# A two-layer attention and feed-forward trunk on one core: for two of four query blocks the product of probabilities and v goes into the block's own score bank

## The chip, the core and the metric

The program runs on one core of one Trainium2 chip, in a single launch. The metric is the time of one execution on the device in microseconds (us). Before the change it is 1463.2 us, the median of three runs (1463.0 to 1464.0). The engines are called as in the profile: PE is TensorE with its weight loads PEld, DVE is VectorE, ACT is ScalarE, POOL is GpSimd, SP is SyncE, which only issues DMAs here.

## What is computed

Two layers over 512 positions and 1024 features, all in float32. The core of one layer:

```python
u = (rmsnorm(x, norm1_w) * (1 + sc1) + sh1) @ w_in     # one combined projection
y_pool, y_conv = pool_mixer(u_pool), b_conv * causal_short_conv(c_conv * u_conv)
o = moba_attention(q, k, v)              # 8 heads of 64, blocks of 256 keys
merged = gates0 * (y_pool @ p_pool) + gates1 * (y_conv @ p_conv) + gates2 * (y_attn @ p_attn)
x = x + g1 * (merged @ w_out)
h2 = rmsnorm(x, norm2_w) * (1 + sc2) + sh2
x = x + g2 * ((silu(h2 @ w_gate) * (h2 @ w_up)) @ w_down)
```

For the change only the attention matters. For each head and each block of 128 queries, the scores of the queries against all earlier keys go through a softmax, the probabilities are transposed, and their product with v is the head's output:

```python
p = softmax(concat([s_sel, s_own]))      # a past block of keys counts where its gate is valid
out = p_sel @ v_sel + p_own @ v_own
```

## The kernel before

Features lie on the 128 partitions, positions along the free axis. A float32 product is made of three matmuls in a faster format (`mm3`): each operand is split into a high and a low part, and high·high, high·low and low·high are added up in the same accumulator. Weights arrive by DMA in a tile `raw` of 8 blocks of 128 x 128, ACT rounds them to `whi` (line 327), DVE makes the rest `wlo` (line 330).

The accumulators (PSUM) are eight banks of 512 float32 per partition, in two pools. `ps_mm()` hands out four single banks, shared by everything that is called `mm` in the profile: the projections, gates and branch products, the transposes and, so far, each product of probabilities and v. `ps_pair()` hands out two tiles of two banks each, called `pair`; in the attention these hold scores, one bank for each of the two heads of a head pair.

The attention is cut into units. A head pair (4 in a layer) and a block of 128 queries (`i` = 0 to 3) make one unit, `unit(hp, i, ...)`, a generator in three stages:

- scores: PE adds a mask and three products of 64 rows for each head into `s = ps_pair()`; DVE takes maxima from `s` (lines 598 to 614), ACT makes the exponentials from it (line 601 for `i` below 2, lines 616 and 618 from 2 on), DVE divides by the sum (line 623);
- transposes: PE transposes the probabilities into one `mm` bank for `i` below 2, into two from `i` = 2 on; ACT copies them rounded (line 634), DVE subtracts for the rest (line 635);
- the product with v (the PV product here): 2(i + 1) matmuls of 128 x 256 into one bank `po`; ACT copies part of it (line 648), DVE adds the other parts (lines 649 and 651), ACT and DVE split the sum for the next product (lines 652 and 653).

The stages are woven into other work. Each time some 2048 columns of `mm3` have been issued, `tick()` lets the generators that are due take a step; the rest of the PE stream is the gate products of the merge (`gate()`, read by ACT at line 912) and the branch products (read by DVE at line 917, `gated`). So between the stages of a unit PE works through gates. `attention` also starts each head pair with eight transposes of q and k (`to_features`, read by ACT at line 517 and DVE at line 518).

PE's instructions keep the order in which they are written; weight splits on DVE are pinned to that order too. For the rest, a scheduler with its own idea of durations fixes, when the program is built, the order of instructions on ACT and DVE and which free bank a new tile gets: a tile takes a bank of its pool that was given up early, and its first matmul waits on PE for the last reader of the tile that was there. Each engine works strictly in its order, so an instruction that waits holds everything behind it.

Of the kernel before, what the change touches and what calls it, by code (L numbers as in the profile page):

```python
# [79 lines left out]
def hybrid_trunk(ctx, tc, xT, ws, ada, cols, pool_w, qk_w, crow, pos, con, out):  # L80
# [12 lines left out]
    def nm(s):  # L93
        uid[0] += 1
        return f"{s}{uid[0]}"
# [4 lines left out]
    def tmp():  # L100
        return work.tile([P, S], F32, tag="tmp", name=nm("tmp"), bufs=5)

    def ps_mm():
        return psum.tile([P, S], F32, tag="mm", name=nm("mm"), bufs=4)

    def ps_pair():
        return psum.tile([P, 2, S], F32, tag="pair", name=nm("pair"), bufs=2)

    def w4(shape, dt=F32):
        return work.tile(shape, dt, tag="w4", name=nm("w4"), bufs=6)  # L110

    def sm(shape, dt=F32, tag="sm", bufs=8):
        return small.tile(shape, dt, tag=tag, name=nm(tag), bufs=bufs)
# [36 lines left out]
    def matmul(*a, **k):  # L150
        tc.keep_in_program_order(T.matmul(*a, **k))  # L151
# [4 lines left out]
    def transpose(*a):  # L156
        tc.keep_in_program_order(T.transpose(*a))  # L157
# [422 lines left out]
    def unit(hp, i, q, k, v, y, nrq, prq):  # L580

        w = P * (i + 1)
        wm = max(w, BLOCK)
        s = ps_pair()

        for a in range(2):
            matmul(s[:, a, i * P:w], ident16, mask, start=True, stop=True)
        for z, (qa, ka) in enumerate(((0, 0), (0, 1), (1, 0))):
            for a in range(2):
                r = slice(a * HD, (a + 1) * HD)  # L590
                matmul(s[:, a, :wm], q[qa][r, i * P:(i + 1) * P], k[ka][r, :wm],
                       start=False, stop=(z == 2), skip_group_check=True)
        cell = lambda: sm([P, 2], tag="asm", bufs=16)
        nsc, sc = nrq[:, i, 2 * hp:2 * hp + 2], prq[:, i, 2 * hp:2 * hp + 2]
        m, nb, den = cell(), cell(), cell()
        pr = [tmp() for _ in range(2)]
        if w <= BLOCK:
            V.tensor_reduce(m, s[:, :, :w], axis=AX.X, op=ALU.max)
            V.tensor_mul(nb, m, nsc)
            for a in range(2):  # L600
                A.activation(pr[a][:, :w], s[:, a, :w], AF.Exp, bias=nb[:, a:a + 1],
                             scale=sc[:, a:a + 1], accum_out=den[:, a:a + 1])
        else:

            gs, pen, mp, nbp, d2 = cell(), cell(), cell(), cell(), cell()
            V.tensor_reduce(gs, s[:, :, :BLOCK], axis=AX.X, op=ALU.add)
            V.tensor_mul(gs, gs, sc)
            V.tensor_scalar(pen, gs, NEG * BLOCK * SCALE, NEG, op0=ALU.is_lt, op1=ALU.mult)
            V.tensor_reduce(mp, s[:, :, :BLOCK], axis=AX.X, op=ALU.max)
            V.tensor_add(mp, mp, pen)  # L610
            V.tensor_reduce(m, s[:, :, BLOCK:w], axis=AX.X, op=ALU.max)
            V.tensor_max(m, m, mp)
            V.tensor_mul(nb, m, nsc)
            V.tensor_add(nbp, nb, pen)
            for a in range(2):
                A.activation(pr[a][:, :BLOCK], s[:, a, :BLOCK], AF.Exp, bias=nbp[:, a:a + 1],  # L616
                             scale=sc[:, a:a + 1], accum_out=den[:, a:a + 1])
                A.activation(pr[a][:, BLOCK:w], s[:, a, BLOCK:w], AF.Exp, bias=nb[:, a:a + 1],  # L618
                             scale=sc[:, a:a + 1], accum_out=d2[:, a:a + 1])
            V.tensor_add(den, den, d2)  # L620
        V.reciprocal(den, den)
        for a in range(2):
            V.tensor_scalar(pr[a][:, :w], pr[a][:, :w], den[:, a:a + 1], None, op0=ALU.mult)
        yield WAIT[i]

        pt = [None] * 2
        for aa in ([0, 1],) if i < 2 else ([0], [1]):
            n = len(aa)
            tp = ps_mm().rearrange("p (j a q) -> p j a q", a=n, q=P)[:, :i + 1]
            for a in aa:  # L630
                for j in range(i + 1):
                    transpose(tp[:, j, a - aa[0], :], pr[a][:, j * P:(j + 1) * P], ident)
            both = w4([P, i + 1, n, 2, P], F32R)
            A.activation(both[:, :, :, 0], tp, AF.Copy)
            V.tensor_sub(both[:, :, :, 1], tp, f32(both)[:, :, :, 0])  # L635
            for a in aa:
                pt[a] = both[:, :, a - aa[0]]
        yield 2

        po = ps_mm().rearrange("p (a h q) -> p a h q", a=2, h=2)  # L640
        for a in range(2):
            for j in range(i + 1):
                matmul(po[:, a].rearrange("p h q -> p (h q)"), v[hp // 2][j][:, hp % 2 * 2 + a].rearrange("p h d -> p (h d)"),
                       pt[a][:, j].rearrange("p h q -> p (h q)"), start=(j == 0), stop=(j == i))
        c = slice(i * P, (i + 1) * P)
        t = tmp()
        part, total = t[:HD, :2 * P].rearrange("p (a q) -> p a q", a=2), t[:, 2 * P:3 * P]
        A.activation(part, po[HD:, :, 0], AF.Copy)
        V.tensor_add(part, part, po[:HD, :, 1])
        for a in range(2):  # L650
            V.tensor_add(total[a * HD:(a + 1) * HD], part[:, a], po[:HD, a, 0])
        A.activation(y[0][:, c], total, AF.Copy)
        V.tensor_sub(y[1][:, c], total, f32(y[0])[:, c])
# [6 lines left out]
    def attention(l, qk, v, nrq, prq, y_attn):  # L660

        for hp in range(PAIRS):
            q = to_features(l, qk, 0, hp)
            yield 1
            k = to_features(l, qk, 1, hp)
            y = bigt(), bigt()
            y_attn.append(y)
            yield 2
            for i in range(TT):
                start(unit(hp, i, q, k, v, y, nrq, prq))  # L670
                if i < TT - 1:
                    yield GAP[i]
            yield 1
# [45 lines left out]
    for l in range(L):  # L719
# [7 lines left out]
        for n, (k, lo, hi) in enumerate([(k, 0, S) for k in range(KT)] if l == 0 else HALVES + REST):  # L727
# [18 lines left out]
            h = norm.k(k)  # L746
# [515 lines left out]
```

## Time and profile before

| | |
|---|---|
| median of 3 runs | 1463.2 us (1463.0 to 1464.0) |
| the profiled execution, its own time | 1463.28 us |
| span of its profile, first to last instruction | 1461.5 us |
| matmuls and weight loads on PE | 8443 each |
| attention of layer 0, of layer 1 (about) | 135 to 308 us, 853 to 1030 us |
| POOL busy | 105.8 us |

The span is 1.8 us shorter than the time of the same execution. In a timeline the columns are start (us from the start of the span), duration, engine, line, operation, what is written and read, shapes, and how many instructions in a row are merged; a bracket at the end is idle time of the engine before it and what ended that. Because all matmuls come from one helper, line 151 stands for every product and the tile names tell them apart: `mm<-w,big` is a PV product, `mm<-ident,w` the transposes of q and k, `mm<-ident,tmp` those of the probabilities, `mm<-big,whi` and `mm<-big,wlo` the gates and branch products, `pair<-mask,ident` and `pair<-big,big` the scores. A matmul's recorded duration is longer than the distance to the next one, since they are pipelined; what a place costs is read from starts.

### The profile page before, as it was taken

How to read it: one execution, taken by the hardware profiler on the slowest of the kernel's cores; microseconds unless marked ns; L12 is line 12 of the kernel's file. 1: busy time of each engine (PE TensorE's matmuls, PEld its weight loads, DVE VectorE, ACT ScalarE, POOL GpSimd, SP SyncE). 2: the span in 40 equal slices, each digit the busy share in tenths (PEclk: the TensorE clock that was granted, in tenths of full speed). 3: DMA queues.
4: the chain of work that ended last, by engine and by line, in shares of the span. 5: the costliest groups of instructions: out<-in, count | busy, mean ns of one | idle time of the engine just before them, and what ended most of it. 6: DMA issues, size and time to landing. Idle time of an engine off the chain costs nothing.

```text
span 1461.5 us, 21960 instructions
## 1 busy us (share of the span) xinstructions
PE 1452.0 (99%) x8443; PEld 1268.2 (87%) x8443; DVE 1053.0 (72%) x1855; ACT 665.8 (46%) x1138; POOL 105.8 (7%) x157
## 2 busy tenths in 40 slices
PE   9999999999999999999999999999999999999998
PEld 7888888788989998989988888778889889989997
DVE  7988888748686867677797867766487757657663
ACT  4634555443454452535444355555335525434450
POOL 0000000001100221210000000000020102111200
PEclk9999999999999999999999999999999999999999
DMA  9645334345436766756545421222462436636522
GB/s 347 225 139 174 124 106 142 133 159 151 109 115 205 200 174 203 187 149 201 189 150 177 159 75 71 73 73 102 154 194 78 142 118 167 175 113 185 138 84 84
DMA packets 84409, 217.19 MB, mean 149 GB/s; under 512 B 10832, under 2 KB 23760, under 8 KB 84304
## 3 DMA queue, kind: packets, MB, share of 16 engines
q1 hardware_dynamic: 67456, 177.37, 35.6%
q0 software_dynamic: 16128, 37.76, 11.8%
q8 instruction: 66, 1.08, 0.3%
q10 hardware_dynamic: 720, 0.66, 0.1%
q14 instruction: 39, 0.32, 0.1%
HBM read 213.65 MB, written 2.10 MB: 148 GB/s over the span
## 4 chain that ended last, share of the span: by engine, by line
PE 95%; DVE 3%; ACT 1%; DMA 1%; issue 0%; SPq 0%
PE mm L151 81%; PE pair L151 12%; PE mm L157 2%; DVE wlo L330 1%; ACT whi L327 0%; DMA w<-in_ada 0%; DMA x<-in_xT 0%; DVE w L376 0%; ACT tmp L616 0%; ACT tmp L618 0%; DVE tmp L485 0%; DVE big L504 0%; DVE big L518 0%; DVE big L488 0%; DVE w L635 0%
## 5 line engine op out<-in xcount | busy, mean ns | idle before, releaser
L151 PE MATMUL mm<-big,whi 128*128 128x512 f32 (+1 forms) x4362 | 1081.2, 339 | 1.6 <-DVE big L488 0.9
L151 PEld LDWEIGHTS mm<-big,whi 128*128 128x128 f32 x4362 | 745.7, 190 | 86.9 <-DVE big L488 1.7
L151 PE MATMUL mm<-big,wlo 128*128 128x512 f32 (+1 forms) x2181 | 736.1, 337 | 0.0
L151 PEld LDWEIGHTS mm<-big,wlo 128*128 128x128 f32 x2181 | 413.9, 190 | 44.4
L327 ACT ACTIVATE whi<-raw 128x1024 fp32r<-128x1024 f32 (+2 forms) x240 | 248.8, 1039 | 283.6 <-PE mm L151 207.5
L330 DVE TENSOR_TENSOR wlo<-raw,whi 128x1024 fp32r<-128x1024 f32 (+2 forms) x240 | 283.6, 1192 | 54.5 <-ACT whi L327 54.2
L327 ACT ACTIVATE whi<-w 128x1024 fp32r<-128x1024 f32 x72 | 76.2, 1059 | 145.4 <-PE mm L151 102.0
L957 DVE SCALAR_TENSOR_TENSOR x<-mm,mod,x 128x512 f32<-128x512 f32 (+1 forms) x90 | 61.7, 688 | 83.2 <-PE mm L151 83.1
L256 POOL DMA_DIRECT2D w<-in_ws x72 | 46.9, 661 | 972.8 <-DVE w L376 391.7
L330 DVE TENSOR_TENSOR wlo<-w,whi 128x1024 fp32r<-128x1024 f32 x72 | 86.8, 1221 | 30.4 <-ACT whi L327 29.7
L376 DVE SCALAR_TENSOR_TENSOR w<-w,csil 128x1024 f32<-128x1024 f32 x80 | 95.9, 1219 | 15.7 <-DMA w<-in_ada 15.5
L151 PE MATMUL pair<-whi,big 128*128 128x512 f32 x224 | 76.8, 390 | 0.0
L258 POOL DMA_DIRECT2D w<-in_ws x72 | 65.0, 930 | 145.1 <-DMA w<-in_ws 131.1
L151 PE MATMUL pair<-big,whi 128*128 128x256 f32 (+1 forms) x376 | 74.0, 294 | 0.0
L151 PEld LDWEIGHTS pair<-big,whi 128*128 128x128 f32 x376 | 60.4, 191 | 2.2
L151 PE MATMUL mm<-whi,big 128*128 128x512 f32 x160 | 57.2, 394 | 1.5 <-ACT big L501 1.2
L151 PE MATMUL pair<-big,wlo 128*128 128x256 f32 (+1 forms) x188 | 55.3, 294 | 0.0
L917 DVE SCALAR_TENSOR_TENSOR big<-big,mm 128x512 f32<-128x512 f32 x48 | 32.6, 684 | 26.4 <-PE mm L151 26.1
L151 PEld LDWEIGHTS pair<-whi,big 128*128 128x128 f32 x224 | 42.1, 188 | 8.7
L515 DVE TENSOR_TENSOR big<-tmp,big 128x512 fp32r<-128x512 f32 x48 | 33.0, 691 | 22.4 <-ACT big L514 21.6
L514 ACT ACTIVATE big<-tmp 128x512 fp32r<-128x512 f32 x48 | 29.7, 623 | 36.1 <-DVE tmp L1096 13.2
L151 PE MATMUL pair<-wlo,big 128*128 128x512 f32 x112 | 43.7, 390 | 0.0
(187 smaller groups left out, 1243.1 us busy)
## 6 DMA issues: line engine op xcount, KB each, us to landing
raw<-in_ws SPq DMA_DIRECT2D x146, 512.0 KB, 3.4
w<-in_ada SPq DMA_DIRECT2D x80, 512.0 KB, 5.1
w<-in_ws POOLq DMA_DIRECT2D x144, 256.0 KB, 4.6
raw<-in_ws SPq DMA_DIRECT2D x64, 256.0 KB, 3.5
raw<-in_ws SPq DMA_DIRECT2D x24, 384.0 KB, 3.5
raw<-in_ada SPq DMA_DIRECT2D x16, 512.0 KB, 3.2
raw<-in_ws SPq DMA_DIRECT2D x16, 448.0 KB, 5.6
raw<-in_ws SPq DMA_DIRECT2D x36, 128.0 KB, 3.0
```

Source lines behind the costliest of these rows:

```text
L151: tc.keep_in_program_order(T.matmul(*a, **k))
L157: tc.keep_in_program_order(T.transpose(*a))
L256: nc.gpsimd.dma_start(dst, self.source(0, 1))
L258: nc.gpsimd.dma_start(dst, self.source(*other), accum_op=ALU.add)
L327: A.activation(hi[:, :n], raw[:, :n], AF.Copy)
L330: ins = V.tensor_sub(lo[:, :n], raw[:, :n], f32(hi)[:, :n])
L376: return V.scalar_tensor_tensor(aw, aw, 1.0, csil, op0=ALU.mult, op1=ALU.mult, accum_out=mod[l][:, part, j:j + 1])
L514: A.activation(hi, src, AF.Copy)
L515: last_split[0] = V.tensor_sub(lo, src, f32(hi))
L917: V.scalar_tensor_tensor(sg, sg, 1.0, branch, op0=ALU.add, op1=ALU.mult)
L957: V.scalar_tensor_tensor(x[k][:, lo:hi], src, mod[l][:, part, k:k + 1], x[k][:, lo:hi], op0=ALU.mult, op1=ALU.add)
```

## The change

For the units with `i` = 2 and `i` = 3 the PV product goes into the first bank of the unit's own score tile `s`. For `i` = 0 and 1 it stays in an `mm` bank. What is computed is the same.

```diff
@@ -637,7 +637,8 @@
                 pt[a] = both[:, :, a - aa[0]]
         yield 2
 
-        po = ps_mm().rearrange("p (a h q) -> p a h q", a=2, h=2)
+
+        po = (s[:, 0] if i >= 2 else ps_mm()).rearrange("p (a h q) -> p a h q", a=2, h=2)
         for a in range(2):
             for j in range(i + 1):
                 matmul(po[:, a].rearrange("p h q -> p (h q)"), v[hp // 2][j][:, hp % 2 * 2 + a].rearrange("p h d -> p (h d)"),
```

The rest of the unit, which reads `po`, is unchanged: the copy, the three additions and the split. There are two such units in each head pair, so 16 in the program: 16 tiles fewer are asked of the `mm` pool. In the program as built, PE, POOL and SP issue the same instructions in the same order; on ACT three copies at line 652 stand one place later, on DVE a few instructions change their turn at two places (lines 635, 651 and 653 in layer 0, lines 917 and 932 in layer 1).

One consequence lies in the score pool. Before, the score tiles alternate between the two buffers. After, the buffers of units 2 and 3 stay taken longer; of the next head pair, units 0 and 1 both get the buffer of unit 2, one after the other, and its unit 2 gets that of unit 3.

## The prediction

> **What bounds the kernel now.** The page is read first: the busy shares, the granted clock, the chain that ended last.
>
> ```profile
> span 1461.5 us, 21960 instructions
> PE 1452.0 (99%) x8443; PEld 1268.2 (87%) x8443; DVE 1053.0 (72%) x1855; ACT 665.8 (46%) x1138; POOL 105.8 (7%) x157
> PEclk9999999999999999999999999999999999999999
> ...
> PE 95%; DVE 3%; ACT 1%; DMA 1%; issue 0%; SPq 0%
> ```
>
> PE is the bound, at full clock, and 95% of the chain is its own work. The change takes no matmul away, so it can only give or take waits of PE. The view of waits, kept to PE, lists what ended them; the rows that belong to accumulator banks in the attention are these:
>
> ```profile
> PE mm L151 <- ACT big L912: 1.0, 2, 0.5
> PE mm L151 <- DVE w L635: 0.3, 1, 0.3
> PE mm L151 <- DVE big L917: 0.2, 1, 0.2
> ```
>
> Four waits, 1.5 us in all. That is a lower bound, since a matmul's recorded duration runs into the gap after it. So I read starts in the timeline of PE. Each head pair after the first puts the PV product of unit 2 right behind four transposes (`mm<-ident,w`), and six sites have the same sequence. Four lines for an undisturbed one, then the three that are not:
>
> ```profile
> 168.74 0.60 PE L157 MATMUL mm<-ident,w 128*128 128x128 f32 x4
> 169.09 0.96 PE L151 MATMUL mm<-w,big 128*128 128x256 f32 x6
> 169.88 0.63 PE L151 MATMUL mm<-big,whi 128*128 128x512 f32 x2
> ...
> 253.26 0.60 PE L157 MATMUL mm<-ident,w 128*128 128x128 f32 x4
> 254.05 0.98 PE L151 MATMUL mm<-w,big 128*128 128x256 f32 x6 [0.19 <-DVE big L917]
> 254.86 0.40 PE L151 MATMUL mm<-big,whi 128*128 128x512 f32 x1
> ...
> 929.15 0.60 PE L157 MATMUL mm<-ident,w 128*128 128x128 f32 x4
> 930.29 0.98 PE L151 MATMUL mm<-w,big 128*128 128x256 f32 x6 [0.54 <-ACT big L912]
> 931.11 0.63 PE L151 MATMUL mm<-big,whi 128*128 128x512 f32 x2
> ...
> 972.79 0.60 PE L157 MATMUL mm<-ident,w 128*128 128x128 f32 x4
> 973.87 0.95 PE L151 MATMUL mm<-w,big 128*128 128x256 f32 x6 [0.48 <-ACT big L912]
> 974.66 0.40 PE L151 MATMUL mm<-big,whi 128*128 128x512 f32 x1
> ```
>
> From the first transpose to the first gate matmul the undisturbed site takes 169.88 − 168.74 = 1.14 us. The others take 1.60, 1.96 and 1.87: they lose 0.46, 0.82 and 0.73.
>
> **What they wait for.** The PV product needs its probabilities and a free `mm` bank. The bracket names the reader whose end let it go, and none of them makes probabilities: line 912 reads a gate, line 917 a branch product. These rows hold the bank:
>
> ```profile
> 253.31 1.28 DVE L917 SCALAR_TENSOR_TENSOR big<-big,mm 128x512 f32<-128x512 f32 x2
> 929.63 0.61 ACT L912 ACTIVATE big<-mm 128x512 f32<-128x512 f32 x1
> 973.05 0.68 DVE L917 SCALAR_TENSOR_TENSOR big<-big,mm 128x512 f32<-128x512 f32 x1
> ```
>
> The first of the two at 253.31 ends near 253.99 (one lasts 0.68, as the third row), 0.06 before PE goes on at 254.05. The second ends at 930.24, 0.05 before 930.29. At 973 the bracket names line 912, but the tile that had this bank before is read by line 917; it ends at 973.73, 0.14 before PE. So all three are waits for a bank, and all three are PV products of units that the change takes out of the `mm` pool.
>
> **The change, part by part.** *The PV product's own wait.* In the score tile the bank was last read by the exponentials, which come before the probabilities, so nothing but the probabilities is left to wait for. They are ready: at 168.74 and its undisturbed fellows the same order runs without a gap. Worth 0.46 + 0.82 + 0.73 = 2.01 us.
>
> *The price of the other bank.* 112 matmuls write, and the readers at lines 648, 649 and 651 read, a `pair` bank. Rows of the same shapes on both pools, here DVE's additions, stand beside each other:
>
> ```profile
> L1067 DVE TENSOR_TENSOR tmp<-tmp,pair 128x256 f32<-128x256 f32 x36 | 15.1, 418 | 2.5 <-ACT tmp L1066 1.8
> L1085 DVE TENSOR_TENSOR tmp<-tmp,mm 128x256 f32<-128x256 f32 x36 | 15.0, 416 | 2.5 <-PE mm L151 2.5
> ```
>
> 418 against 416 ns: nothing.
>
> *The fourth wait,* which follows the second at once, is no PV product:
>
> ```profile
> 935.20 0.40 PE L151 MATMUL mm<-big,wlo 128*128 128x512 f32 x1
> ...
> 935.89 0.40 PE L151 MATMUL mm<-big,wlo 128*128 128x512 f32 x1
> 936.56 0.74 PE L151 MATMUL mm<-big,whi 128*128 128x512 f32 x2 [0.27 <-DVE w L635]
> 937.13 0.40 PE L151 MATMUL mm<-big,wlo 128*128 128x512 f32 x1
> ```
>
> Three matmuls take 0.69 (935.20 to 935.89), here 1.24: 0.55 lost. The bank is that of unit 3's transposes, read by line 635, which still holds in the changed program. If PE comes 0.82 earlier and line 635 does not, the 0.82 is lost again here. So I follow line 635 back:
>
> ```profile
> 932.85 0.40 DVE L649 TENSOR_TENSOR tmp<-tmp,mm 64x256 f32<-64x256 f32 x1
> 933.29 0.57 DVE L651 TENSOR_TENSOR tmp<-tmp,mm 64x128 f32<-64x128 f32 x2
> 933.90 0.31 ACT L652 ACTIVATE big<-tmp 128x128 fp32r<-128x128 f32 x1 [2.15 <-DVE tmp L651]
> 934.11 1.04 ACT L327 ACTIVATE whi<-raw 128x1024 fp32r<-128x1024 f32 x1
> 935.18 1.09 ACT L634 ACTIVATE w<-mm 128x512 fp32r<-128x512 f32 x2
> 935.81 1.29 DVE L635 TENSOR_TENSOR w<-mm,w 128x512 fp32r<-128x512 f32 x2 [1.28 <-ACT w L634]
> ```
>
> ACT idles 2.15 us for line 651, and behind it wait the weight rounding (line 327) and then line 634. Line 651 ends at 933.86 whatever PE does: line 649 before it has no bracket, so DVE came straight from other work. In the changed order line 327 stands ahead of line 652. I assume that it needs a weight buffer that PE leaves with the gate just before, and so starts some 1.0 us earlier, at 933.1; the view can't name that wait, because line 652 held ACT longer. It then ends near 934.1, line 652 fits behind it, and line 634 starts near 934.35 instead of 935.18. Line 635 is then 0.8 to 0.9 earlier and PE 0.82: the wait stays, and I take it as smaller by 0.1. Bounds: it grows by 0.82 (the gain of the second site gone), or it vanishes (0.55 more). The middle is taken because the new order lets ACT follow PE.
>
> *What the score bank holds up.* Two new waits. First, the next head pair's unit 0 waits for unit 2's line 651. The closest site, and the site with the closest second wait, unit 1 behind unit 0's exponentials in the same buffer:
>
> ```profile
> 258.38 0.57 DVE L651 TENSOR_TENSOR tmp<-tmp,mm 64x128 f32<-64x128 f32 x2
> 261.34 0.28 PE L151 MATMUL pair<-mask,ident 128*128 128x128 bf16 x2
> ...
> 223.62 0.20 ACT L601 ACTIVATION_READ_ACCUMULATOR tmp<-pair,asm,nrq 128x1 f32 x1
> 225.88 0.28 PE L151 MATMUL pair<-mask,ident 128*128 128x128 bf16 x2
> ```
>
> The first has 261.34 − 258.95 = 2.39 us of room. PE comes 0.46 earlier, and in the changed order one line 635 (0.65, half of 1.29) goes ahead of line 651, which leaves about 1.3. The second has 225.88 − 223.82 = 2.06. Gates cover both, and nothing on DVE or ACT is queued behind these waits, as they stand on PE. If the cover went, every microsecond beyond the room would be a microsecond of the end. Cost here: 0.
>
> *After the attention* PE runs back to back again, so what it gains there is kept. SP's and POOL's queues are issued in the same order; nothing is moved past them.
>
> **The sum.** −2.01 − 0.1 = −2.1 us. The profiled execution took 1463.28, its span and 1.8 around it; the median of the runs is 0.1 less. 1463.28 − 2.1 gives 1461.2 us, 0.14% less than before. A difference of 0.2% (2.9 us) is about what a measurement of this kernel can tell from no change, so this counts as within.
>
> The Trainium skill, "Perfetto Trace Analysis" (section Matmuls), speaks against the edit: independent products should rotate through different banks, so that evacuating one overlaps the next. By that rule the PV product should stay in the rotation. By it the change would gain nothing, 1463.3, or lose as in the slower rival below; by the rows, which show three waits inside the rotation and 1.3 us or more of room outside it, the sum stays 1461.2.
>
> **The rivals.** *Given back at the next wait.* The fourth wait grows by 0.82, or the gates behind the other two sites run into a bank that DVE frees no earlier, since DVE is busy without PE's help there. For: line 651 above did not depend on PE. Against: after 254.86 and 974.66 there is no further wait in the list. With the second site lost, 0.46 + 0.73 = 1.2 remain: 1462.1; with all lost 1463.3.
>
> *Slower: the score products stall.* The place is unit 1 behind unit 0's exponentials, at three head pairs in each layer; it decides once ACT and DVE bring the exponentials later by more than the room, 2.06 us at its closest. With the same room at all six, a delay of 3 us would cost 6 × 0.94 = 5.6 and give 1466.8. Against: the exponentials would have to slip by more than three additions and a weight split together, and nothing is added to either queue.
>
> *All bank waits go, and more.* With the fourth gone too: 2.01 + 0.55 = 2.56, 1460.7. The largest version takes the short gap that PE shows after each block of probability transposes:
>
> ```profile
> 934.65 0.71 PE L151 MATMUL mm<-big,whi 128*128 128x512 f32 x2
> 935.43 0.62 PE L151 MATMUL mm<-big,whi 128*128 128x512 f32 x2
> ```
>
> The first pair, behind transposes, is 0.09 longer than the second; with 32 units that is 2.9 us, and 1463.28 − 2.1 − 2.9 = 1458.3. The Trainium skill, "Perfetto Trace Analysis" (section Optimization Strategy), says that a gap which repeats on the saturated engine can mean that accumulator space for the next tile is short. Against it: the gap has this one size, while a wait for a reader varies, as the 0.46 to 0.82 above do.
>
> **How the numbers follow.** Forecast 1461.2, own range 1460.6 to 1461.9: 0.60, all within 0.2%. Given back, 1461.9 to 1463.4: 0.19, within. More than forecast: 0.15, of which 0.11 beyond 2.9 us. Slower: 0.06, of which 0.05 beyond. So faster 0.11, same 0.84, slower 0.05. The range reaches from 1460.0 (the fourth wait gone as well, and the 0.2 to 0.8 by which runs scatter) to 1463.3 (everything given back).
>
> **What would show it.** Right: the three brackets behind `mm<-ident,w` are gone, each of the six sites takes 1.14 us, line 912 and line 917 leave PE's list of waits, and line 635's wait near 936 is a little shorter. Wrong: `pair<-mask,ident` waits for line 651 or line 601; or the wait for line 635 grows to over 1 us; or the readers on `pair` are longer than on `mm`; or the gap behind the transposes shrinks.

## The result and the profile after

The changed kernel takes 1461.18 us (median of 22 runs, 1460.71 to 1462.01); the kernel before, run beside it, 1463.3 us (22 runs, 1462.82 to 1464.0). The ratio is 0.9986, with a 95% interval of 0.998 to 0.9992, which leaves out 1. The forecast was 1461.2. The profiled execution took 1461.3 us, its span and 1.8 us around it, as before.

The page of the changed kernel, the busy shares, the granted clock and the chain that ended last:

```profile
span 1459.5 us, 21946 instructions
PE 1451.3 (99%) x8443; PEld 1267.9 (87%) x8443; DVE 1053.5 (72%) x1855; ACT 665.8 (46%) x1138; POOL 105.9 (7%) x157
PEclk9999999999999999999999999999999999999999
...
PE 96%; DVE 2%; DMA 1%; ACT 1%; issue 0%; SPq 0%; ACTq 0%
```

PE still bounds the kernel, at the same clock, with the same 8443 matmuls; its share of the chain rose from 95% to 96%. The lines from 640 on have numbers one higher than before (line 917 is now 918, 651 is 652). The view of waits of the changed kernel, kept to PE and cut to the attention of layer 1, has one row left of the three rows for banks; cut to the attention of layer 0 it has none:

```profile
PE mm L151 <- DVE w L635: 0.2, 1, 0.2
```

The timeline of PE at the three sites that had waited (start, duration, what, how many):

```profile
253.24 0.60 PE L157 MATMUL mm<-ident,w 128*128 128x128 f32 x4
253.59 0.95 PE L151 MATMUL pair<-w,big 128*128 128x256 f32 x6
254.39 0.40 PE L151 MATMUL mm<-big,whi 128*128 128x512 f32 x1
...
928.86 0.60 PE L157 MATMUL mm<-ident,w 128*128 128x128 f32 x4
929.21 0.95 PE L151 MATMUL pair<-w,big 128*128 128x256 f32 x6
930.01 0.40 PE L151 MATMUL mm<-big,whi 128*128 128x512 f32 x1
...
971.59 0.60 PE L157 MATMUL mm<-ident,w 128*128 128x128 f32 x4
971.94 0.95 PE L151 MATMUL pair<-w,big 128*128 128x256 f32 x6
972.73 0.40 PE L151 MATMUL mm<-big,whi 128*128 128x512 f32 x1
```

The brackets are gone and the product now writes `pair`. From first transpose to first gate matmul the sites take 1.15, 1.15 and 1.14 us; before they took 1.60, 1.96 and 1.87. That is 0.45 + 0.81 + 0.73 gained (0.72 for the third by the differences of starts below).

To see where else time went I subtracted the start of each matmul in one trace from the start of the same matmul in the other. This gives PE's lead over the kernel before, and it changes in steps. Besides the three steps above there are three smaller ones.

*Near 258, 0.10 gained, not foreseen.* The eight transposes of unit 3's probabilities are one merged row before and one after; its duration is all that shows. The first fence is the kernel before, the second the changed one:

```profile
257.60 1.14 PE L157 MATMUL mm<-ident,tmp 128*128 128x128 f32 x8
...
257.28 0.75 DVE L518 SCALAR_TENSOR_TENSOR big<-mm,colt,big 128x512 fp32r<-128x512 f32 x1
```

```profile
257.12 1.04 PE L157 MATMUL mm<-ident,tmp 128*128 128x128 f32 x8
```

Before, the second four of them got the bank that line 518 reads until 257.28 + 0.75 = 258.03, and the first of these four starts at 258.08 in the trace, 0.05 behind it. This is a fifth wait for a bank, and merging had hidden it.

*Near 935, 0.08 gained.* The wait that was to stay, in the changed kernel on PE, ACT and DVE:

```profile
934.78 0.40 PE L151 MATMUL mm<-big,wlo 128*128 128x512 f32 x1
935.37 0.72 PE L151 MATMUL mm<-big,whi 128*128 128x512 f32 x2 [0.20 <-DVE w L635]
935.94 0.40 PE L151 MATMUL mm<-big,wlo 128*128 128x512 f32 x1
...
932.71 1.06 ACT L327 ACTIVATE whi<-raw 128x1024 fp32r<-128x1024 f32 x1 [1.78 <-PE mm L151]
933.68 0.29 ACT L653 ACTIVATE big<-tmp 128x128 fp32r<-128x128 f32 x1
934.00 1.09 ACT L634 ACTIVATE w<-mm 128x512 fp32r<-128x512 f32 x2
...
934.63 1.29 DVE L635 TENSOR_TENSOR w<-mm,w 128x512 fp32r<-128x512 f32 x2 [0.33 <-ACT w L634]
```

The three matmuls from 934.78 to 935.94 take 1.16 us, where the same three took 1.24 before and undisturbed ones take 0.69. Line 327 now shows the bracket that the profile before could not show: it waits for PE, so it comes earlier when PE does, and line 635 with it.

*At 843.7, the start of layer 1, 0.33 lost.* Here the changed kernel has a wait that the one before has not. The rows of the changed kernel:

```profile
833.59 0.33 SPq L400 DMA_DIRECT2D w<-in_ada  x1
838.69 1.23 DVE L376 SCALAR_TENSOR_TENSOR w<-w,csil 128x1024 f32<-128x1024 f32 x1 [0.55 <-DMA w<-in_ada]
843.12 0.42 DVE L889 TENSOR_TENSOR big<-mm,big 128x256 fp32r<-128x256 f32 x1 [0.45 <-ACT big L888]
843.16 0.39 PE L151 MATMUL mm<-big,wlo 128*128 128x512 f32 x1
843.70 0.63 PE L157 MATMUL mm<-ident,w 128*128 128x128 f32 x4
```

The first transposes of q need the bank that line 889 reads until 843.54. DVE is late because line 376 stood 0.55 us for a weight transfer, issued at 833.59, and everything behind it on DVE, line 889 too, moved with it. The wait is in no row of the list of waits; only the difference of starts shows it. Whether the change brings it is a question for the runs below.

The prices of the other bank, rows grouped by shape of the changed kernel (busy us, then mean ns of one):

```profile
L650 DVE TENSOR_TENSOR tmp<-tmp,mm 64x256 f32<-64x256 f32 x16 | 6.6, 410 | 8.3 <-ACT tmp L649 8.1
L650 DVE TENSOR_TENSOR tmp<-tmp,pair 64x256 f32<-64x256 f32 x16 | 6.5, 409 | 14.3 <-ACT tmp L649 14.3
```

409 against 410 ns: reading `pair` costs nothing.

### The profile page after: what moved, and what is told of

Read it like the earlier page. It is cut to its first block, busy times and chain, and to the rows that moved or that the text cites. A ratio compares the mean times of both kernels' runs of the same rounds, so it can differ in the third digit from the quotient of the medians.

```text
span 1459.5 us, 21946 instructions
## 1 busy us (share of the span) xinstructions
PE 1451.3 (99%) x8443; PEld 1267.9 (87%) x8443; DVE 1053.5 (72%) x1855; ACT 665.8 (46%) x1138; POOL 105.9 (7%) x157
## 4 chain that ended last, share of the span: by engine, by line
PE 96%; DVE 2%; DMA 1%; ACT 1%; issue 0%; SPq 0%; ACTq 0%
PE mm L151 82%; PE pair L151 13%; PE mm L157 2%; DVE wlo L330 1%; DMA w<-in_ada 0%; DMA x<-in_xT 0%; DVE w L376 0%; ACT whi L327 0%; DVE tmp L485 0%; DVE big L504 0%; DVE big L488 0%; ACT big L487 0%; ACT big L491 0%; DVE tmp L476 0%; DVE big L477 0%
```

## The experiments

Ten runs were made, eight kernels and the changed one twice more. The edits are against the changed kernel. The table gives each median with its ratio to the kernel before and the 95% interval, and the steps of PE's lead over the kernel before in its profile (plus for gained; good to about 0.02). `e3` has further steps, all losses, which its section gives. The medians of the kernel before lie at 1463.3 in all comparisons. rep1 and rep2 are single executions.

| | median us (runs) | ratio, interval | 254 | 258 | 844 | 930 | 935 | 973 |
|---|---|---|---|---|---|---|---|---|
| the change | 1461.18 (22) | 0.9986, 0.998 to 0.9992 | +0.45 | +0.10 | −0.33 | +0.81 | +0.08 | +0.72 |
| three | 1461.11 (11) | 0.9985, 0.9976 to 0.9994 | +0.45 | +0.10 | −0.27 | +0.81 | +0.07 | +0.72 |
| thirteen | 1463.21 (11) | 1.0, 0.9991 to 1.0008 | 0 | 0 | −0.09 | 0 | 0 | 0 |
| e3 | 1464.18 (11) | 1.0005, 0.9996 to 1.0014 | +0.45 | +0.10 | −0.08 | +0.81 | +0.07 | +0.72 |
| tp0 | 1460.69 (11) | 0.9981, 0.9972 to 0.999 | +0.45 | +0.10 | −0.10 | +0.81 | +0.57 | +0.72 |
| tpb | 1462.82 (11) | 0.9996, 0.9988 to 1.0005 | 0 | +0.10 | 0 | 0 | +0.57 | 0 |
| ordr | 1460.55 (11) | 0.9981, 0.9973 to 0.999 | +0.45 | +0.09 | 0 | +0.81 | +0.57 | +0.72 |
| tf | 1460.92 (11) | 0.9983, 0.9974 to 0.9992 | +0.45 | +0.10 | 0 | +0.81 | +0.09 | +0.72 |
| best | 1460.62 (11) | 0.9983, 0.9973 to 0.9992 | +0.45 | +0.10 | 0 | +0.81 | +0.57 | +0.72 |
| rep1 | 1460.87 (1) | | +0.45 | +0.10 | 0 | +0.81 | +0.08 | +0.72 |
| rep2 | 1460.96 (1) | | +0.45 | +0.10 | 0 | +0.81 | +0.08 | +0.72 |

### Only the three that waited, and only the other thirteen

`three` numbers the units in the order in which they start and lets only units 10, 22 and 26 use the score bank:

```diff
+    serial, GAP = [0], (2, 3, 3, 3)
...
+        w, site, serial[0] = P * (i + 1), serial[0], serial[0] + 1
...
-        po = (s[:, 0] if i >= 2 else ps_mm()).rearrange("p (a h q) -> p a h q", a=2, h=2)
+        po = (s[:, 0] if site in (10, 22, 26) else ps_mm()).rearrange("p (a h q) -> p a h q", a=2, h=2)
```

> Only the three PV products that waited (254, 930 and 974 us in the profile before) go into their score bank; the other thirteen of units 2 and 3 go back to the mm banks. Theory (the whole gain is three waits for a shared bank): everything of the change is kept, PE is ahead by 0.45 behind the first site, and by 0.79 and 0.72 more behind the others; 1461.2 us, 2.0 less than before. Rival (the gain is a general relief of the shared banks, spread over sixteen units): about 3/16 of it, 0.4 us, 1462.9.

`thirteen` is the complement, with the same numbering:

```diff
+        po = (s[:, 0] if i >= 2 and site not in (10, 22, 26) else ps_mm()).rearrange("p (a h q) -> p a h q", a=2, h=2)
```

> The other thirteen PV products of units 2 and 3 go into their score banks, the three that waited stay in mm banks. Theory (three waits): the three brackets of 0.19, 0.54 and 0.48 us behind the transposes of q and k are back, each of these sites takes 1.60, 1.96 and 1.87 us again, no gain, 1463.3. Rival (spread relief): 13/16 of 2.0, 1461.6.

The medians were 1461.11 and 1463.21: all of the gain and none of it. The timeline of PE in `thirteen` has the three waits back (the last two rows are DVE's):

```profile
253.87 0.98 PE L151 MATMUL mm<-w,big 128*128 128x256 f32 x6 [0.19 <-DVE big L918]
930.22 0.98 PE L151 MATMUL mm<-w,big 128*128 128x256 f32 x6 [0.55 <-ACT big L913]
973.77 0.95 PE L151 MATMUL mm<-w,big 128*128 128x256 f32 x6 [0.48 <-DVE asm L620]
...
972.95 0.68 DVE L918 SCALAR_TENSOR_TENSOR big<-big,mm 128x512 f32<-128x512 f32 x1
973.54 0.15 DVE L620 TENSOR_TENSOR asm<-asm,asm 128x2 f32<-128x2 f32 x1
```

So the gain is these three waits (with the 0.10 and the 0.08 that come after them), and thirteen of the sixteen moved products change nothing. The last bracket names line 620, which reads no bank, where the profile before named line 912 at the same place: a bracket names who finished last before the start, and the reader that counts has to be found by the bank. Here it is line 918. PE has a semaphore instruction of its own for DVE there, which begins at 973.66 in the trace: line 918 has ended by then (972.95 + 0.68 = 973.63), line 620 has not (973.69). In the kernel before it is the same, with the instruction at 973.77 between the end of line 917 at 973.73 and that of line 620 at 973.80.

### Other tiles leave the shared banks instead

`tpb` takes as many tiles out of the shared banks, but the transposes of the first head; the PV products go back:

```diff
-            tp = ps_mm().rearrange("p (j a q) -> p j a q", a=n, q=P)[:, :i + 1]
+            tp = (s[:, 0] if i >= 2 and aa == [0] else ps_mm()).rearrange("p (j a q) -> p j a q", a=n, q=P)[:, :i + 1]
...
-        po = (s[:, 0] if i >= 2 else ps_mm()).rearrange("p (a h q) -> p a h q", a=2, h=2)
+        po = ps_mm().rearrange("p (a h q) -> p a h q", a=2, h=2)
```

> Sixteen tiles leave the shared banks, as in the change, but others: the probability transposes of the first head of units 2 and 3 go into the unit's score bank, the PV products stay in mm banks as before. Theory (only the tile that waits counts): the wait for line 635 near 936 goes, 0.5 us as the run that moved both showed (PE 0.57 further ahead there, of which 0.08 the change had already), and the three waits of the PV products at 254, 930 and 974 stay with 0.46, 0.82 and 0.73: 1462.8. Rival (the number of tiles in the shared banks is what counts): as much as the change, 1461.2.

1462.82, as expected. The steps are 0.10 and 0.57, and the three large waits stay. The number of tiles in the pool does not set the time; the one bank that a tile gets does.

### All four units in their score bank

```diff
-        po = (s[:, 0] if i >= 2 else ps_mm()).rearrange("p (a h q) -> p a h q", a=2, h=2)
+        po = s[:, 0].rearrange("p (a h q) -> p a h q", a=2, h=2)
```

> All four units of a head pair put the PV product into their score bank, so sixteen more tiles leave the shared pool. Theory (what counts is when the one bank comes free that the next tile gets): the scores of unit 3 then need the buffer of unit 1, whose last addition ends later than these scores start today, by 0.21 us near 161, 0.91 near 246, 0.53 near 289, and by about 0.4 and 0.2 near 924 and 968; with 0.05 for the way from DVE to PE each, 2.5 us of new waits behind the line of the additions, of which 0.3 is not felt, since the wait at the start of layer 1 that the change brought (844) then goes: 1463.4 (1463.0 to 1463.8), the change's gain all lost. Rival (each product taken out of the shared banks helps): 1461.2 or less.

It takes 1464.18, 3.0 us more than the changed kernel: the gain is lost, and more, and the time lies above the expected range of 1463.0 to 1463.8. The list of PE's waits has a new row:

```profile
PE pair L151 <- DVE tmp L652: 1.8, 4, 0.8
```

PE and DVE at the largest of them, in the timeline:

```profile
247.21 0.28 PE L151 MATMUL pair<-mask,ident 128*128 128x128 bf16 x2 [0.80 <-DVE tmp L652]
...
246.59 0.56 DVE L652 TENSOR_TENSOR tmp<-tmp,pair 64x128 f32<-64x128 f32 x2
```

The scores of unit 3 wait for the last addition of unit 1, which ends at 246.59 + 0.56 = 247.15. This is the slower rival's end (scores that stall), at another pair of units. The six steps lost are 0.45, 0.29, 0.96, 0.59, 0.50 and 0.23, together 3.02. Five of them I had expected with 2.5, and they measure 2.57. The first, at 150.9, was not on my list, and neither was a loss of 0.10 at the first gate behind the third site, near 975. At 150.9 line 651 ended at 150.74 before and the scores began at 150.85, 0.11 of room; in this profile DVE was 0.49 later. That goes back to a weight rounding on ACT that waits for its transfer, here in the kernel before and in `e3`:

```profile
140.51 1.06 ACT L327 ACTIVATE whi<-raw 128x1024 fp32r<-128x1024 f32 x1 [1.58 <-DMA raw<-in_ws]
```

```profile
141.06 1.06 ACT L327 ACTIVATE whi<-raw 128x1024 fp32r<-128x1024 f32 x1 [2.15 <-DMA raw<-in_ws]
```

It starts 0.55 later, and DVE is some 0.5 behind from there to the addition. In the ten other profiles, measured from PE's own time, the same addition ends 0 to 0.43 later than in the kernel before, within 0.01 of it in both repeats of the change. So how much of the 0.45 an execution of `e3` loses should depend on that transfer; there is one profile of `e3`, so this was not seen.

### The wait that the change left

`tp0` keeps the change and adds the first head's transposes to the score bank (the `tp` lines of `tpb` alone):

> The change, and besides it the probability transposes of the first head of units 2 and 3 go into the same score bank, which the exponentials have left. Theory: the one bank wait that the change left in the attention (line 635 near 935, 0.25 us between starts beyond an undisturbed 0.69) goes too, no new wait comes, and the PV product still finds its bank free as line 635 has read it by then: 0.25 less than the changed kernel, 1460.9. Rival (the PV product now waits for line 635 of its own unit, on which its probabilities depend anyway): no difference from that, 1461.2; rival (score buffers held longer delay the scores of the next head pair): 1461.5 or more.

`ordr` leaves the banks as the change has them and alters ACT's order: the weight rounding that stood ahead of unit 2's copy is issued after it (`site` numbers the units as in `three`; `latch` starts as `[None]`).

```diff
-        A.activation(hi[:, :n], raw[:, :n], AF.Copy)
+        with tc.issue_after(latch[0].ins) if latch[0] is not None else nullcontext(): A.activation(hi[:, :n], raw[:, :n], AF.Copy); latch[0] = None
...
-        A.activation(y[0][:, c], total, AF.Copy)
+        ins = A.activation(y[0][:, c], total, AF.Copy); latch[0] = ins if site == 22 else None
```

> The change, and on ACT the weight rounding (line 327) that stands ahead of unit 2's copy (line 653) at 932.7 in the changed kernel is made to come after it; as built it then stands behind unit 3's two copies of line 634 too. The banks are those of the change. Theory (what is left of the wait near 935 is line 634 standing behind a weight rounding, 1.06 us long): line 634 and with it line 635 come some 0.6 us earlier and the wait of about 0.5 us between starts goes: 1460.7. Rival (line 635 is held by DVE's own work, or the rounding that is now late stops the gate that needs it): 1461.2, or above it by what the rounding is late, up to 1 us.

Both took the whole wait, 0.57 where the change alone has 0.08; the medians are 1460.69 and 1460.55. `tp0` had expected 0.25 less than the changed kernel and got 0.49: what the change had left was 1.16 − 0.69 = 0.47, not 0.25. The rows of `ordr`, ACT, DVE and PE:

```profile
932.60 0.60 ACT L913 ACTIVATE big<-mm 128x512 f32<-128x512 f32 x1 [2.03 <-PE mm L151]
...
933.46 1.07 ACT L634 ACTIVATE w<-mm 128x512 fp32r<-128x512 f32 x2
...
934.08 1.29 DVE L635 TENSOR_TENSOR w<-mm,w 128x512 fp32r<-128x512 f32 x2 [0.19 <-ACT w L634]
...
933.20 0.71 PE L151 MATMUL mm<-big,whi 128*128 128x512 f32 x2
...
933.98 0.62 PE L151 MATMUL mm<-big,whi 128*128 128x512 f32 x2
...
934.67 0.62 PE L151 MATMUL mm<-big,whi 128*128 128x512 f32 x2
```

The product that waited starts at 934.67, before the first line 635 has ended (one lasts 0.68, so 934.76). So it cannot have waited for it, and my expectation that the banks stay those of the change was wrong: in the program as built this product now gets the bank of the gate that line 913 reads, since line 913 too came forward on ACT, and is done with it at 933.20. The trace agrees: the weight load of this product waits for ACT alone, where in the changed kernel it waits for DVE. The time is as forecast, but `ordr` is a second test of the bank, not one of ACT's order. An order changed on one engine changed the choice of a bank. That a rounding ahead of line 634 decides the size of this wait is therefore only argued, from the rows of the changed kernel; it was not tried with the bank held fixed.

### The start of layer 1

`tf` gives the first transposes of q of a layer a bank of the score pool:

```diff
-        pt = ps_mm()
+        pt = ps_pair()[:, 0] if which == 0 and hp == 0 else ps_mm()
```

> The change, and the first transposes of q of each layer go into a bank of the score pool instead of an mm bank. Theory: at 843.7 in the changed kernel these transposes wait 0.3 us for line 889, which reads v from their bank; the score buffers have been read by 841.2, so the wait goes and nothing else changes: 0.1 to 0.35 less than the changed kernel (the wait was 0.08 to 0.33 in the profiles so far), 1460.9. Rival: the next product takes the bank that is read late, and waits in the transposes' place: 1461.2.

Its profile happens to have a transfer as late as in the changed kernel's, and PE passes:

```profile
843.23 0.42 DVE L889 TENSOR_TENSOR big<-mm,big 128x256 fp32r<-128x256 f32 x1 [0.45 <-ACT big L888]
...
843.39 0.60 PE L157 MATMUL pair<-ident,w 128*128 128x128 f32 x4
```

The transposes start at 843.39, though line 889 ends only at 843.65. The median, 1460.92, is 0.26 below the change's, less than the intervals tell apart. The changed kernel twice more:

> The changed kernel once more, for the place at the start of layer 1 (843.7) where its first profile gave back 0.33 us to a wait for line 889. Theory (the wait is the landing time of a weight transfer in front of DVE's line 376, which differs between executions): less than 0.33 or nothing here, with the three steps of 0.45, 0.81 and 0.72 unchanged. Rival (the lead of PE itself runs into DVE's work): 0.33 again, within 0.03.

> The same as rep1, a third execution. Theory: a step between 0 and 0.35 that differs from both others, and with it the start of line 376 behind the issue of its transfer (4.71 us before, 5.10 in the first profile after). Rival: 0.33 each time.

Neither repeat lost anything there. `rep1`, DVE and PE:

```profile
838.11 1.23 DVE L376 SCALAR_TENSOR_TENSOR w<-w,csil 128x1024 f32<-128x1024 f32 x1
842.55 0.42 DVE L889 TENSOR_TENSOR big<-mm,big 128x256 fp32r<-128x256 f32 x1 [0.45 <-ACT big L888]
...
843.04 0.39 PE L151 MATMUL mm<-big,wlo 128*128 128x512 f32 x1
843.27 0.60 PE L157 MATMUL mm<-ident,w 128*128 128x128 f32 x4
```

From the issue of its transfer to the start of line 376 it took 5.10 us in the first profile of the change, 4.64 in `rep1` (issued at 833.47) and 4.71 before. The other profiles without the edit of `tf` or of `best` follow the same order: 5.05 in `three`, which lost 0.27; 4.85 to 4.87 in `thirteen`, `e3` and `tp0`, which lost 0.08 to 0.10; at most 4.70 in `tpb`, `ordr` and `rep2`, which lost nothing. The 0.33 belongs to that execution; a lead over the kernel before does not bring it by itself. My expectation that rep2 would differ from both others missed: like rep1 it lost nothing.

### Together

`best` is `tp0` with the edit of `tf`.

> The change, the first head's transposes of units 2 and 3 in the score bank, and the first transposes of q of each layer in a bank of the score pool. Theory: no wait for a bank is left in either attention nor at the start of layer 1; 0.1 to 0.3 less than 1460.7, which the first two gave: 1460.5. Rival as in the last: 1460.7.

1460.62, no better than `tp0` or `ordr`, as the rival had it. Its profiled execution (1462.03) lost 1.46 us at one place outside the attention, where the others lost nothing; the chain of waits there (start, duration, what):

```profile
495.31 5.59 DMA w<-in_ws
...
505.20 0.34 DVE tmp L1086
...
505.58 0.50 PE mm L151 x2
```

A weight transfer of 5.59 us leads to line 1086, for which PE waits; in the other eleven profiles the same transfer took 4.0 to 4.6 us. By the medians, `ordr`, `best` and `tp0` are the fastest versions, 2.8, 2.7 and 2.6 us below the kernel before; against the changed kernel the intervals overlap, and only the step near 935 in the traces says that they are half a microsecond ahead.

## Why the prediction was right

*The bound.* Right: PE at 99%, no matmul taken away, and every step of the gain is a wait of PE.

*Three waits for a bank, 2.01.* Right: they measure 0.45 + 0.81 + 0.72 = 1.98. `three` and `thirteen` show that these products alone bring it, and `tpb` that it is not a matter of how many tiles share the banks. Naming line 917 and not the bracket's line 912 as the reader at 973 is borne out by `thirteen`, where the bracket changes its name and the wait stays, and by PE's semaphore instruction.

*The price of the other bank, nothing.* Right, 409 against 410 ns.

*The fourth wait, smaller by 0.1.* Right in size, 0.08. The assumption that line 327 waits for PE is shown by its bracket; it started at 932.71, 0.4 earlier than assumed. Of that, 0.29 is PE's lead from layer 0, which the prediction carried into neither side: line 635 came 1.18 earlier (934.63 for 935.81) and PE 1.11 (934.78 for 935.89), where it had 0.8 to 0.9 and 0.82. Only the difference counts, and the 0.1 was taken as a middle between bounds of 0.82 lost and 0.55 gained, so that it fits this well is in part luck. Whether ACT's order alone decides stays open, since `ordr` changed the bank as well.

*New waits of the scores, none here.* Right. The closest place behind the last addition, PE and DVE of the changed kernel:

```profile
260.76 0.28 PE L151 MATMUL pair<-mask,ident 128*128 128x128 bf16 x2
...
259.00 0.56 DVE L652 TENSOR_TENSOR tmp<-tmp,pair 64x128 f32<-64x128 f32 x2
```

The room is 260.76 − 259.56 = 1.20 us; 1.3 was predicted from 2.39. `e3` shows that this point was worth working out: where the room is 0.91 too small, 0.96 is lost.

*After the attention what is gained is kept.* Mostly right. Without the edit of `tf`, two profiles lost 0.33 and 0.27 at the start of layer 1, three lost 0.08 to 0.10, two of them with no gain left to lose (`thirteen` and `e3`), and four lost nothing, both repeats among them. The prediction had not considered that place. The kernel before passed with little to spare: line 888 done at 843.35 + 0.42 = 843.77, transposes at 844.01, and some 0.15 of the 0.24 between is what PE needs there behind DVE:

```profile
843.35 0.42 DVE L888 TENSOR_TENSOR big<-mm,big 128x256 fp32r<-128x256 f32 x1 [0.45 <-ACT big L887]
...
844.01 0.60 PE L157 MATMUL mm<-ident,w 128*128 128x128 f32 x4
```

*What the sum left out.* The 0.10 near 258. The repeats' steps, 0.45 + 0.10 + 0.81 + 0.08 + 0.72 = 2.16, put the change at 1463.3 − 2.16 = 1461.1; the forecast of 2.1 lacked the 0.10 and had 0.05 too much in the others. It also lacked the 0 to 0.33 that is lost at the start of layer 1 from one execution to the next. These stand against each other, and PE's own start differs by some tenths of a us between the profiles before any attention, so that the forecast meets the median to 0.02 us is luck; that it meets it to a few tenths is not.

*The rivals.* Given back at the next wait: did not happen. Scores that stall: not in the change, but in `e3`. All bank waits go: not by the change, but `tp0` and `ordr` make it happen, with 1460.7 predicted and 1460.69 and 1460.55 measured. The larger version, that the gap behind probability transposes is a shortage of banks, falls: in `ordr`, with no bank wait left around it, the first three gate matmuls behind them take 933.98 − 933.20 = 0.78 us and the next three 0.69, the same 0.09, and in the trace the matmul behind the gap waits for no semaphore. What the gap is stays open. The Trainium skill, "Perfetto Trace Analysis" (section Optimization Strategy), says only that a repeating gap can mean a shortage, and here it does not.

By the rotation rule of the Trainium skill, "Perfetto Trace Analysis" (section Matmuls), as the prediction applied it, the change should have gained nothing. The runs bear it out for products whose next bank is in use, in `e3`, and go against it at three sites, where the bank that the rotation offered came free later than the score bank.

## What to carry to other kernels

Before moving a tile to another accumulator bank, list for each instance the time at which the last reader leaves the old and the new bank beside the time at which PE arrives: the gain is the sum of the positive gaps on the old side and the loss the same sum on the new side, and most instances are in neither. Then do the same for the tiles that come after, as far as the program as built gives them other banks: in `ordr` and near 258 the gain came from such a tile. Read waits from differences of starts, also inside merged rows, since the list of waits showed 1.5 us of bank waits where 2.7 could be removed (0.45 + 0.10 + 0.81 + 0.57 + 0.72). A step that one profile shows behind a transfer should be seen in a second execution before it is put down to a change.

## What the runs showed that was not expected

PE goes on at a fixed distance behind the reader that it waited for, and there are two such distances. In the kernel before, behind line 917 at 254 and line 912 at 930, it is 0.05 to 0.06 us, and so it is behind line 652 in `e3` (247.15 to 247.21). Behind line 917 at 973 before (973.73 to 973.87) and line 889 at 843.7 after (843.54 to 843.70) it is 0.14 to 0.16. At all other waits of PE that the twelve profiles list it is 0.05 to 0.06, and with the long distance there is each time a semaphore instruction of 0.05 us of its own on PE ahead of the weight load, as at 973 above. It is not the number of semaphores: in `e3` weight load and matmul at 247 wait for one each, and PE goes on after 0.06. No run shows whether the extra instruction makes the whole of the difference.

The landing of one and the same weight transfer differed by at least 0.46 us between two executions of one program (5.10 and 4.64 us from issue to use), as much as a whole wait that the change removes. How much the wait at 843.7 costs in each profile went with that landing.
